# Both conditions' opening modulations on VectorE, and a list schedule with traced durations and a shared port

## The chip, the cores and the metric

The kernel runs on one core of one Trainium2 chip. The metric is the device time of one execution in microseconds. Before the change it is 1679.93 us, the median of three runs (1679.58 to 1681.09). The engines are called PE (TensorE matmuls), PEld (its weight loads), DVE (VectorE), ACT (ScalarE), POOL (GpSimd) and SP (SyncE, whose queue SPq issues nearly all DMAs).

## The reference

Two layers of a diffusion backbone over 512 latent and 256 context tokens of width 1024. Each layer is a token mixer and a gated convolutional FFN, each behind an RMSNorm whose result is modulated with a shift and a scale, and gated. Latent tokens take their modulation from the vector `c`, context tokens from `c_ctx`: both go through the same weights.

```
m  = silu(c) @ w_ada[i] + b_ada[i]                 # shift, scale, gate, twice: 6 x 1024
cm = silu(c_ctx) @ w_ada[i] + b_ada[i]             # the same for the context
h  = rmsnorm(x)  * g * (1 + scale)  + shift
hc = rmsnorm(xc) * g * (1 + cscale) + cshift
layer 0: o, oc = gated linear attention(h, hc)     # 4 heads, decays, state over chunks
layer 1: o     = latent attention(h, hc)           # 8 heads, low-rank keys and values
x = x + gate * o;   x = x + gate2 * conv_ffn(modulate(x))    # context alike, in layer 0
```

The output is the latent stream, (1, 512, 1024) in fp32.

## The kernel before

Activations lie feature-major: a feature tile is 128 features on the partitions by 768 tokens (512 latent, 256 context). Weights and activations are split into a high part (rounded to fp32r by ACT) and a low part (the rest, a subtraction on DVE), and a product is three matmuls: high by high, high by low, low by high. So each weight tile passes a DMA (`ws`), an ACT cast (`wh`) and a DVE subtraction (`wl`), through rings of three buffers, before PE uses it. In the trace all recorded instructions have one line, 263, that of the call that emits them.

The stages are: the opening (`start`, L562), the four heads of gated linear attention (`gla`, L712), the output projection and the first FFN, the latent attention, and the second FFN.

**The opening.** It loads x and the first weights, forms each token's scale `rb` (squares on ACT, sums `sacc` on DVE, `ssq` and `rows` on PE, a power `nr` on POOL), and for each of eight feature tiles makes the two modulations (scale and shift) for the two conditions (`dots`, L623). For tiles 1, 2 and 4 (`MOD_PE`) they are small matmuls `adp`. For tiles 0, 3, 5, 6 and 7 a modulation is a sum over 1024 products of a weight row and the condition, `cb`: in one DVE pass (`junk`, with an accumulator read after it), or, for the entries of `MOD_POOL`, as a product on POOL (`prod`) that ACT then sums. Nine of the twenty are on POOL, all for condition 1, the context; five more entries of the table are of tiles that PE handles and have no effect. Then `normed` scales the tile (DVE writes `x`, ACT writes `hh`, DVE writes `hl`), and PE multiplies it with the first weights: queries `Gq`, keys `Gk`, output gates `mr` and decay gates `mu`, for the latent tokens; the context's products come later, and its last ones go to the bank `both`. Tiles 0 to 7 of x are called x_92 to x_99 in the program, the modulation weights wa_100 (tile 0) to wa_119 (tile 6).

**The heads.** For each head `gates` makes from `Gz` the running sums of log decays (a scan on DVE) and from them `Q` and `K`, for two directions; `values` makes `vps` (copied to `v` by ACT); `core` transposes K (`ktp`, copied to `KT`), makes scores `scp`, states `stp` -> `R` (DVE), outputs `ops`, norms them (`o` on DVE) and transposes them (`Got`). Projections of the next head (`G`) are woven between. In the same stretch 32 modulations of the other chunks are made on DVE and 32 on POOL (`wa<-wa,cb`).

**What sets the order.** `Later` (L102) records each instruction of a stage, and when a pool closes emits all by a list schedule (`flush`, L198): every engine takes the first recorded of the instructions that its own clock shows as ready, with a duration from `cost` (L175) and a delay between engines. Only the order comes out of it; the waits follow from the data. An engine runs its instructions strictly in that order. The costs hold for the whole program: a duration that is too short there puts an instruction into an engine's queue ahead of others that could have run while it waits.

Of the kernel before, what the change touches and what calls it, by code (L numbers as in the profile page):

```python
# [18 lines left out]
P = 128  # L19
# [11 lines left out]
# columns of the vector table  # L31
# [14 lines left out]
# columns of the table of constants  # L46
# [6 lines left out]
# how the start is divided: feature tiles whose first modulations are products of the tensor engine, and  # L53
# (tile, shift or scale, condition) of those whose products GpSimd makes
MOD_PE = (1, 2, 4)
MOD_POOL = (
    (0, 0, 1), (0, 1, 1), (1, 0, 0), (1, 0, 1), (1, 1, 0), (2, 1, 0), (3, 0, 1), (3, 1, 1), (4, 0, 1), (5, 0, 1),
    (5, 1, 1), (6, 0, 1), (7, 0, 1), (7, 1, 1),
)
MOD_STAGE = (0, 1, 2)  # tiles whose modulation weights come in the buffers of the other weights  # L60
# what arrives in turn: modulation weights of a feature tile, two tiles of the first weights, the context
START_LOADS = ("m0", "m1", "w0", "w1", "w2", "m3", "m2", "m5", "m4", "ctx", "w3", "m7", "m6")
COND_AFTER = (3, 7)  # tiles of squares after which the two conditions are taken
CTX_NORM = 5  # the step of the first products at which the norm of the context comes
CTX_LAG = 5  # steps of the context behind those of the latent tokens, not before its norm
NORM_POOL = (3, 6)  # the feature tiles of a latent norm that GpSimd and ScalarE modulate


def weave(*streams):
    """Emits the steps of several streams in proportion: (generator, its expected total, where it starts).  # L70
    A step is its time on the tensor engine, or its share of the total."""
    live = [[g, total, sum(start)] for g, total, *start in streams]
    while live:
        s = min(live, key=lambda x: x[2])
        try:
            step = next(s[0])
            s[2] += step[0] if isinstance(step, tuple) else step / s[1]
        except StopIteration:
            live.remove(s)


def paced(units):
    """Steps of units of work that count as equally long: (generator, its expected total)."""
# [18 lines left out]
class Later:  # L102
    """Records instructions and emits them when a pool ends, in the order of a list schedule.

    Every engine takes the first recorded of the instructions whose operands and buffers are ready; the costs are
    those of the guide. Only the order comes from here: Tile finds all waits anew, in the instructions so ordered."""
# [3 lines left out]
    def __init__(self, tc):  # L110
        self.tc, self.real = tc, tc.nc
        self.ops, self.preload = [], None
        self.seen = {}  # tile -> its accesses in this batch
        self.done = {}  # tile -> when its accesses end, from earlier batches
        self.held, self.tags = {}, {}  # tag, and tile of it -> (tag, the tiles in its buffers)
        self.old = {}  # tile -> the one before in its buffer
        self.free = dict.fromkeys(self.ENGINES, 0.6) | {"sync": 2.2}
        self.table = None
        # from the end of an instruction on one engine to the start of one that needs it on another
# [21 lines left out]
    def record(self, engine, op, args, kw):  # L141
        if op == "preload_act_table_set":
            # goes before the next activation, if that changes the table
            self.preload = args
            return
# [3 lines left out]
        for x, write in aps:  # L149
            row = math.prod(x.tensor.shape[1:])  # L150
            lo = hi = x.offset % row
            # the elements of a partition: from lo to hi, and if they are few, which
# [19 lines left out]
        self.ops.append((engine, op, args, kw, preload, deps, {x.name for x, _ in aps}, *self.cost(engine, op, args, kw, aps)))  # L172

    @staticmethod
    def cost(engine, op, args, kw, aps):  # L175
        """time on the engine, and the activation table"""
# [4 lines left out]
        if engine == "tensor":  # L181
            if op == "transpose":
                return max(0.107, x.shape[-1] / 2400.0), None
            full = (args[1] if len(args) > 1 else kw["lhsT"]).dtype == F32
            return (max(0.213, n / 600.0) if full else max(0.107, n / 2400.0)), None
# [5 lines left out]
        n = max(math.prod(y.shape[1:]) for y, _ in aps)  # L191
        if engine == "vector":
# [3 lines left out]
        return (0.16 * n if kw.get("op") == ALU.pow else 0.1 + n / 450.0), None  # L196

    def flush(self):  # L198
# [6 lines left out]
        # a tile takes the oldest buffer that is no longer in use, and waits for all accesses to the tile there  # L205
# [21 lines left out]
        queue = {e: [] for e in self.ENGINES}  # nothing left to wait for: when ready, which  # L227
        heap = {e: [] for e in self.ENGINES}  # ready by now
# [8 lines left out]
        while any(queue.values()) or any(heap.values()):  # L237
# [6 lines left out]
            cost, table = ops[i][7:]  # L244
# [3 lines left out]
            self.free[e] = end[i] = t + cost  # L248
            plan.append((t, len(plan), i))
# [5 lines left out]
        assert len(plan) == count, "instructions wait for each other"  # L255
# [11 lines left out]
class Net:  # L267
# [36 lines left out]
    def ffn_order(gi):  # L304
        """pairs of a group of FFN features, woven with the down products of the group before"""
# [25 lines left out]
    def ahead(self, n):  # L331
        """n weights after those in use are on their way"""
# [5 lines left out]
    def get(self, key, ahead=2):  # L338
        """the split weights of this key"""
# [6 lines left out]
    def split(self, hi, lo, src, engine=None):  # L346
        """hi + lo == src exactly, each with 12 significant bits."""
# [4 lines left out]
    def weight(self, key, src, shape, pool=None):  # L352
        """split weights, in the ring of 3 or in a pool that keeps them"""
# [1211 lines left out]
def _rope(np):  # L1565
    """cos | signed sin of the axial rotary embedding for the 512 latent tokens"""
    f = 16
# [89 lines left out]
```

## Time and profile before

| what | value |
|---|---|
| median of three runs | 1679.93 us |
| span of the profiled execution, first to last instruction | 1679.1 us |
| PE busy | 1611.4 us, 96% |
| DVE busy | 1116.0 us, 66% |
| ACT busy | 720.4 us, 43% |
| POOL busy | 298.9 us, 18% |
| mean granted clock of TensorE | 0.989 |

The profiled execution is known by its span; the median of the runs lies 0.83 us above it, and so does about what an execution has around its instructions. Busy times are unions over the span, so they don't add up over engines. A matmul's own length in the trace overlaps with that of the next; the distance of two starts says what one costs. A DVE row's length includes any time for which the instruction has been issued and does not get on.

### The profile page before, as it was taken

To read this page: it belongs to the slowest core of one execution; us is meant where nothing else is said; L and a number is where in the kernel's file an instruction comes from. 1 tells how busy PE (TensorE), PEld (TensorE's weight loads), DVE (VectorE), ACT (ScalarE), POOL (GpSimd) and SP (SyncE) were. 2 spreads that over 40 slices of the span, in tenths; PEclk is the share of its full clock that TensorE was granted. 3 is DMA by queue.
4 is the path that set the end of the run, shared out by engine and by line. 5 is a ranking of instruction groups with operands and counts; after the bars stand their busy time and mean duration, and the time that the engine had idled before them with its cause. 6 is when DMAs were issued, how large, how long until landed. Compare 5 with 4: busy or idle time off the path is not lost.

```text
span 1679.1 us, 22918 instructions
## 1 busy us (share of the span) xinstructions
PE 1611.4 (96%) x9086; PEld 1386.0 (83%) x9086; DVE 1116.0 (66%) x1773; ACT 720.4 (43%) x1253; POOL 298.9 (18%) x170
## 2 busy tenths in 40 slices
PE   7899889889999999999999999999999999999999
PEld 4688778778888888888888888788889888888887
DVE  7977777885677855655544567777776765555554
ACT  4555444552443533323322336666653533333331
POOL 3223233330112411111100020334400100000000
PEclk9999999999999999999999999999999999999999
DMA  8222223233133343333331222100031232232232
GB/s 320 99 93 96 93 86 111 76 116 142 38 113 121 131 151 126 126 126 126 126 101 64 76 109 79 40 15 26 20 120 47 69 113 98 90 101 99 90 100 76
DMA packets 50079, 165.59 MB, mean 99 GB/s; under 512 B 5554, under 2 KB 7346, under 8 KB 49972
## 3 DMA queue, kind: packets, MB, share of 16 engines
q1 hardware_dynamic: 49332, 162.04, 28.2%
q0 software_dynamic: 640, 2.10, 0.3%
q8 instruction: 71, 1.16, 0.3%
q14 instruction: 36, 0.29, 0.1%
HBM read 159.92 MB, written 4.19 MB: 98 GB/s over the span
## 4 chain that ended last, share of the span: by engine, by line
PE 78%; DVE 10%; issue 5%; ACT 3%; DMA 2%; POOL 1%; SPq 0%; POOLq 0%; DVEq 0%; ACTq 0%
PE G L263 59%; PE Gs L263 4%; PE av L263 2%; PE ukv L263 2%; DVE K L263 2%; PE Gu L263 2%; DVE junk L263 2%; PE uq L263 1%; DMA wa<-in_wada 1%; PE pt L263 1%; DVE hl L263 1%; PE ops L263 1%; PE vps L263 1%; DVE R L263 1%; PE stp L263 1%
## 5 line engine op out<-in xcount | busy, mean ns | idle before, releaser
L263 PE MATMUL G<-hh,wh 128*128 128x512 f32 (+1 forms) x1416 | 507.0, 358 | 1.2 <-DVE x L263 1.2
L263 PE MATMUL G<-hl,wh 128*128 128x512 f32 (+2 forms) x1416 | 494.1, 350 | 0.2 <-DVE hl L263 0.2
L263 PE MATMUL G<-hh,wl 128*128 128x512 f32 (+1 forms) x1400 | 491.9, 351 | 0.0
L263 DVE TENSOR_TENSOR wl<-ws,wh 128x1024 fp32r<-128x1024 f32 (+3 forms) x178 | 222.4, 1251 | 270.2 <-ACT wh L263 268.7
L263 ACT CAST wh<-ws 128x1024 fp32r<-128x1024 f32 (+3 forms) x186 | 189.5, 1020 | 441.9 <-PE G L263 422.8
L263 PEld LDWEIGHTS G<-hh,wh 128*128 128x128 f32 x1416 | 267.4, 189 | 36.3 <-DVE x L263 1.4
L263 PEld LDWEIGHTS G<-hl,wh 128*128 128x128 f32 (+1 forms) x1416 | 266.7, 188 | 36.9 <-DVE hl L263 0.7
L263 PEld LDWEIGHTS G<-hh,wl 128*128 128x128 f32 x1400 | 264.3, 189 | 34.5
L263 POOL TENSOR_TENSOR wa<-wa,cb 128x1024 f32<-128x1024 f32 x64 | 168.4, 2634 | 524.3 <-DVE mod L263 263.2
L263 PE MATMUL G<-ph,wh 128*128 128x512 f32 (+1 forms) x512 | 181.8, 355 | 2.3 <-DVE z L263 2.3
L263 PE MATMUL G<-ph,wl 128*128 128x512 f32 (+1 forms) x512 | 182.1, 356 | 0.0
L263 PE MATMUL G<-pl,wh 128*128 128x512 f32 (+1 forms) x512 | 181.7, 355 | 0.0
L263 DVE SCALAR_TENSOR_TENSOR z<-G,vec,z 128x511 f32<-128x511 f32 x248 | 151.0, 651 | 1.7 <-ACT z L263 0.9
L263 DVE CUSTOM_DVE_ANT_0 junk<-wa,cb 128x1024 bf16<-128x1024 f32 x75 | 109.9, 1465 | 49.2 <-DMA wa<-in_wada 49.0
L263 PEld LDWEIGHTS G<-ph,wh 128*128 128x128 f32 x512 | 96.2, 188 | 16.9 <-issue 2.6
L263 PEld LDWEIGHTS G<-pl,wh 128*128 128x128 f32 x512 | 96.1, 188 | 14.8
L263 PEld LDWEIGHTS G<-ph,wl 128*128 128x128 f32 x512 | 96.1, 188 | 13.9
L263 ACT ACTIVATE wa<-wa 128x1024 f32<-128x1024 f32 x64 | 67.6, 1057 | 66.4 <-POOL wa L263 66.3
L263 DVE SCALAR_TENSOR_TENSOR x<-G,mod,x 128x512 f32<-128x512 f32 (+1 forms) x112 | 64.8, 610 | 35.2 <-PE G L263 34.7
L263 ACT ACTIVATE z<-G,vec 128x768 f32<-128x768 f32 (+1 forms) x82 | 72.4, 883 | 3.1 <-PE G L263 2.3
L263 ACT ACTIVATE z<-z 128x768 f32<-128x768 f32 (+1 forms) x44 | 32.5, 739 | 93.2 <-DVE z L263 93.2
L263 DVE SCALAR_TENSOR_TENSOR y<-G,mod,y 128x512 f32<-128x512 f32 (+1 forms) x72 | 49.2, 688 | 21.3 <-PE G L263 20.7
(343 smaller groups left out, 2673.0 us busy)
## 6 DMA issues: line engine op xcount, KB each, us to landing
wa<-in_wada SPq DMA_DIRECT2D x90, 512.0 KB, 3.5
ws<-in_wup SPq DMA_DIRECT2D x88, 512.0 KB, 3.3
ws<-in_wdn SPq DMA_DIRECT2D x44, 512.0 KB, 3.5
ws<-in_win SPq DMA_DIRECT2D x13, 512.0 KB, 3.3
ws<-in_wmd SPq DMA_DIRECT2D x9, 512.0 KB, 3.3
ws<-in_wv SPq DMA_DIRECT2D x8, 512.0 KB, 3.7
ws<-in_wog SPq DMA_DIRECT2D x8, 512.0 KB, 3.6
ws<-in_womh SPq DMA_DIRECT2D x8, 512.0 KB, 5.6
```

The lines of the kernel that those rows point to most:

```text
L263: getattr(getattr(self.real, engine), op)(*args, **kw)
```

## The change

Three edits. `MOD_POOL` is empty, so all twenty opening modulations of tiles 0, 3, 5, 6 and 7 are DVE passes. In `start` the pass for condition 1 is recorded right behind that for condition 0 of the same tile (`dots(k, 1)`), not five steps later with the context. And `Later` gets other durations (matmuls some 3 to 8% longer, DVE's scan with about twice its time, POOL's power with a fixed part), and a port: an instruction of DVE or POOL for which `shares` is true starts, in the plan, no earlier than the end of the last such instruction of the other engine. A message for a stuck plan is longer. Comments are gone, so line numbers differ (L263 is L282).

```diff
-MOD_POOL = (
-    (0, 0, 1), (0, 1, 1), (1, 0, 0), (1, 0, 1), (1, 1, 0), (2, 1, 0), (3, 0, 1), (3, 1, 1), (4, 0, 1), (5, 0, 1),
-    (5, 1, 1), (6, 0, 1), (7, 0, 1), (7, 1, 1),
-)
+MOD_POOL = ()
...
+        self.port = {"vector": 0.0, "gpsimd": 0.0}
...
             if op == "transpose":
-                return max(0.107, x.shape[-1] / 2400.0), None
+                return 0.109, None
             full = (args[1] if len(args) > 1 else kw["lhsT"]).dtype == F32
-            return (max(0.213, n / 600.0) if full else max(0.107, n / 2400.0)), None
+            return (max(0.22, n / 590.0) if full else max(0.109, 0.0063 + n / 2296.0)), None
...
+        if op == "tensor_tensor_scan":
+            return 0.07 + n / 480.0, None
...
-        return (0.16 * n if kw.get("op") == ALU.pow else 0.1 + n / 450.0), None
+        return (0.9 + 0.17 * n if kw.get("op") == ALU.pow else 0.1 + n / 450.0), None
+
+    @staticmethod
+    def shares(engine, op, aps):
+
+        reads = [x for x, write in aps if not write and x.space != PSUM and math.prod(x.shape[1:]) > 1]
+        if engine == "gpsimd":
+            return bool(reads) and op != "dma_start"
+        fast = op in ("tensor_scalar", "tensor_copy") and aps[0][0].space != PSUM
+        return engine == "vector" and (len(reads) > 1 or bool(reads) and fast)
...
-            cost, table = ops[i][7:]
+            cost, table, shares = ops[i][7:]
+            if shares:
+
+                t = max(t, self.port[e])
...
             self.free[e] = end[i] = t + cost
+            if shares:
+                self.port["gpsimd" if e == "vector" else "vector"] = t + cost
...
         for k in range(KT + CTX_LAG):
             if k < KT:
                 dots(k, 0)
+                dots(k, 1)
...
             if k >= CTX_LAG:
-                dots(k - CTX_LAG, 1)
                 normed(k - CTX_LAG, 1, *CTX)
```

What this moves is seen in the order of each engine. First DVE in the opening, at feature tile 3: `wa_107` and `wa_108` are its scale and shift weights, `junk` is a modulation pass, `wl` a low part of weights, x_93 and x_95 are feature tiles 1 and 3. Before:

```order
L263 ISA junk,mod_68<-wa_107,cb 128x1024
L263 ISA mod_68 128x1
L263 CAST wh<-wl 128x2x32
L263 ISA junk,mod_68<-wa_108,cb 128x1024
L263 ISA mod_68 128x1
L263 TENSOR_SCALAR mod_68<-adp,vec 128x2 x2
L263 TENSOR_SCALAR gain_123<-mod_68,vec 128x2
L263 TENSOR_TENSOR mod_68<-mod_68,vec 128x2
L263 SCALAR_TENSOR_TENSOR x_93<-x_93,gain_123,rb 128x512
```

The same place on DVE now:

```order
L282 ISA junk,mod_68<-wa_107,cb 128x1024
L282 ISA mod_68 128x1
L282 TENSOR_SCALAR gain_123<-mod_68,vec 128x1
L282 ISA junk,mod_68<-wa_108,cb 128x1024
L282 ISA mod_68 128x1
L282 TENSOR_TENSOR wl<-firsts,wh 128x1024
L282 TENSOR_TENSOR mod_68<-mod_68,vec 128x2
L282 ISA junk,mod_68<-wa_107,cb 128x1024
L282 ISA mod_68 128x1
L282 TENSOR_SCALAR mod_68<-adp,vec 128x2 x2
L282 TENSOR_SCALAR gain_123<-mod_68,vec 128x2
```

A second pass over wa_107 has come in (one over wa_108 follows after x_95), and the weights' low part stands between; POOL's products are gone from its own queue.

Second, PE in the second head, between the transpositions of the keys of the two directions (K_756 and K_762 before, K_738 and K_744 now); `G` are projections of the next head. Before:

```order
L263 MATMUL ktp<-kon,K_756 128x128 x6
L263 MATMUL G<-hl,wh 128x512
L263 MATMUL G<-hh,wl 128x512
L263 MATMUL ktp<-kon,K_762 128x128 x6
L263 MATMUL stp<-v,KT_782 128x256
L263 MATMUL scp<-Q_755,K_756 128x128
```

Now:

```order
L282 MATMUL ktp<-kon,K_738 128x128 x6
L282 MATMUL G<-hh,wh 128x512
L282 MATMUL G<-hl,wh 128x512
L282 MATMUL G<-hh,wl 128x512
L282 MATMUL G<-hh,wh 128x512
L282 MATMUL G<-hl,wh 128x512
L282 MATMUL G<-hh,wl 128x512
L282 MATMUL G<-hh,wh 128x512
L282 MATMUL G<-hl,wh 128x512
L282 MATMUL G<-hh,wl 128x512
L282 MATMUL G<-hh,wh 128x512
L282 MATMUL G<-hl,wh 128x512
```

The second six transpositions (K_744) come only after these eleven projections, one state and 14 more projections, where two stood before. In the fourth head the same pair has 37 projections between them where it had nine.

Third, ACT in the first head, about the second copy of values out of PSUM; `t`, `Q` and `K` are steps of the gates, `wa` sums a POOL product. Before:

```order
L263 ACTIVATE t_666<-t_666 128x768 x2
L263 ACTIVATE cf_663<-cf_663 128x6
L263 ACTIVATE Q_661<-K_662 128x768
L263 ACTIVATE wa,mod_68<-wa 128x1024
L263 ACTIVATE K_662<-K_662 128x768
L263 COPY v<-vps 128x512
```

Now:

```order
L282 ACTIVATE t_648<-t_648 128x768 x2
L282 ACTIVATE wa,mod_68<-wa 128x1024
L282 COPY v<-vps 128x512
L282 ACTIVATE cf_645<-cf_645 128x6
L282 ACTIVATE Q_643<-K_644 128x768
```

The copy has moved ahead of the three steps that wait for DVE's scan; the sum of the POOL product still stands before it.

## Rows read from the trace of the kernel before

**Rows 1.** The page: span; an engine's busy us, share, instructions.

```profile
span 1679.1 us, 22918 instructions
PE   1611.4 (96%) x9086; PEld 1386.0 (83%) x9086; DVE 1116.0 (66%) x1773; ACT 720.4 (43%) x1253; POOL 298.9 (18%) x170
```

**Rows 2.** Windows by stage: length; busy us of each engine; PE clock, DMA share, GB/s.

```profile
13.00:81.20 68.20, 54.57 (x304) 41.49 (x305) 63.02 (x106) 32.69 (x59) 27.09 (x11) 0.97 0.52 195
81.20:384.00 302.80, 271.93 (x1684) 244.44 (x1683) 233.98 (x347) 150.14 (x263) 93.02 (x36) 0.95 0.30 103
384.00:1000.00 616.00, 611.17 (x3529) 537.00 (x3529) 373.21 (x543) 215.69 (x276) 95.86 (x47) 1.00 0.32 109
1000.00:1330.00 330.00, 321.45 (x2041) 276.88 (x2040) 243.26 (x530) 192.68 (x493) 82.48 (x74) 0.99 0.16 51
1330.00:1679.00 349.00, 345.14 (x1528) 283.67 (x1526) 197.74 (x242) 121.32 (x151) 0.00 (x0) 1.00 0.29 95
```

**Rows 3.** POOL's timeline, opening, first head: start, length, instruction, idle before and releaser.

```profile
23.59 2.41 POOL L263 TENSOR_TENSOR prod<-wa,cb 128x1024 f32<-128x1024 f32 x1 [1.85 <-ACT prod L263]
...
64.84 2.61 POOL L263 TENSOR_TENSOR prod<-wa,cb 128x1024 f32<-128x1024 f32 x1 [3.63 <-ACT prod L263]
91.69 3.55 POOL L263 TENSOR_TENSOR wa<-wa,cb 128x1024 f32<-128x1024 f32 x1 [24.23 <-DVE mod L263]
```

**Rows 4.** DVE's timeline, opening.

```profile
13.19 3.44 DVE L263 CUSTOM_DVE_ANT_0 junk<-wa,cb 128x1024 bf16<-128x1024 f32 x1
...
21.56 0.75 DVE L263 SCALAR_TENSOR_TENSOR x<-x,gain,rb 128x512 f32<-128x512 f32 x1 [2.08 <-ACT rb L263]
...
23.64 2.38 DVE L263 TENSOR_TENSOR mod<-mod,vec 128x2 f32<-128x2 f32 x1
...
27.96 1.21 DVE L263 CUSTOM_DVE_ANT_0 junk<-wa,cb 128x1024 bf16<-128x1024 f32 x1
29.11 0.08 DVE L263 DVE_READ_ACCUMULATOR2_ANT mod<- 128x1 f32 x1
...
65.10 2.38 DVE L263 TENSOR_TENSOR mod<-mod,vec 128x2 f32<-128x2 f32 x1
...
70.16 0.74 DVE L263 SCALAR_TENSOR_TENSOR hl<-x,mod,hh 128x512 fp32r<-128x512 f32 x1
```

**Rows 5.** POOL's groups, opening, heads: busy, mean ns; idle before.

```profile
L263 POOL TENSOR_TENSOR prod<-wa,cb 128x1024 f32<-128x1024 f32 x9 | 24.2, 2690 | 30.4 <-ACT prod L263 18.2 <-ACT cb L263 12.3
L263 POOL TENSOR_TENSOR wa<-wa,cb 128x1024 f32<-128x1024 f32 x32 | 86.4, 2701 | 200.7 <-DVE mod L263 170.2 <-ACT t L263 12.8 <-ACT wa L263 6.6
```

**Rows 6.** PE's timeline, opening and heads.

```profile
13.33 1.87 PE L263 MATMUL ssq<-ones,sacc 128*128 128x1 f32 x8 [2.70 <-DVE sacc L263]
...
80.95 0.40 PE L263 MATMUL Gz<-U,w 128*128 128x512 f32 x1
...
99.77 0.41 PE L263 MATMUL vps<-wh,hh 128*128 128x256 f32 x1 [3.12 <-ACT v L263]
...
177.02 1.54 PE L263 MATMUL ktp<-kon,K 128*128 128x128 f32 x6 [4.53 <-DVE K L263]
...
333.87 0.70 PE L263 MATMUL stp<-v,KT 128*128 128x256 f32 x2 [3.40 <-ACT KT L263]
```

**Rows 7.** Windows behind three of these waits, columns as in rows 2.

```profile
100.00:105.00 5.00, 5.00 (x31) 5.00 (x31) 4.01 (x8) 1.90 (x3) 0.00 (x0) 0.66 0.21 79
175.00:180.00 5.00, 2.98 (x13) 2.80 (x13) 4.73 (x5) 2.75 (x7) 1.77 (x2) 0.51 0.18 50
335.00:340.00 5.00, 4.28 (x20) 3.95 (x21) 2.77 (x6) 2.02 (x5) 0.00 (x0) 0.66 0.54 187
```

**Rows 8.** DVE's groups in the heads, columns as in rows 5.

```profile
L263 DVE TENSOR_TENSOR K<-K,k 128x768 f32<-128x768 f32 x8 | 15.6, 1959 | 0.6 <-ACT K L263 0.6
L263 DVE TENSOR_TENSOR_SCAN K<-keep,Q 128x768 f32<-128x768 bf16 x8 | 14.0, 1751 | 0.1
L263 DVE TENSOR_TENSOR K<-K,md 128x768 f32<-128x768 f32 x8 | 7.6, 953 | 0.2
```

More of the change, by code (lines that the diff above doesn't have):

```diff
@@ L171, in record @@
             preload, self.preload = self.preload, None
-        self.ops.append((engine, op, args, kw, preload, deps, {x.name for x, _ in aps}, *self.cost(engine, op, args, kw, aps)))
+        self.ops.append((engine, op, args, kw, preload, deps, {x.name for x, _ in aps}, *self.cost(engine, op, args, kw, aps), self.shares(engine, op, aps)))
     @staticmethod
@@ L254, in flush @@
                     release(j)
-        assert len(plan) == count, "instructions wait for each other"
+        if len(plan) != count:
+            stuck={i for i in range(count) if left[i]>0}
+            i=min(stuck); path=[]
+            while i not in path:
+                path.append(i); i=min(j for j in deps[i] if end[j]==0.0)
+            raise AssertionError("\n".join(f"{i} {ops[i][0]} {ops[i][1]} {sorted(ops[i][6])}" for i in path[path.index(i):]))
         for name, l in users.items():
```

## The prediction

> **What bounds the kernel now.** First the page's totals: PE is busy 1611.4 of 1679.1 us [rows 1], so at most the other 68 us and time at a low clock can be won. Then the windows by stage, which say where those lie [rows 2]: between 384 and 1000 and from 1330 on PE idles 5 and 4 us, and order can do next to nothing there. In the opening (13 to 81.2) PE idles 13.6 us, and DVE is busy 63.0 of 68.2: DVE sets the end there. In the four heads (81.2 to 384) PE idles 30.9 of 302.8 us, at a mean granted clock of 0.95, while DVE is busy 234: neither is full, they wait for each other. In the latent attention (1000 to 1330) PE idles 8.6 us.
>
> Next the timelines of POOL and DVE in the opening, side by side [rows 3, 4]. A pass of DVE over 1024 elements takes 1.21 us, 1.15 from its start to the next instruction (27.96 to 29.11). But an addition on two columns, issued at 23.64, takes 2.38 us and ends at 26.02, when POOL's product (23.59 + 2.41) ends at 26.00; another, issued at 65.10, ends at 67.48, POOL's at 67.45. So a DVE instruction issued while a POOL product runs does not get on until the product ends. Eight of the nine products hold DVE like this, the first in the pass at 13.19 (3.44 us), the last at 65.10; the ninth falls into a wait for `rb`.
>
> **The opening, part by part.** Removed: nine POOL products of 2.69 us [rows 5] and nine ACT sums; neither engine is the bound here, so these count nothing by themselves. What counts is the eight holds on DVE. The pass at 13.19 loses 3.44 - 1.21 = 2.2, the two additions about 2.2 each, and so on: some 2.1 each, 17 us in all. Not all of it comes back: the instruction behind the first pass needs `ssq`, which PE finishes at 13.33 + 1.87 = 15.2 [rows 6], while the pass would end at 14.4, so 1 us stays as idle time. In turn the scale chain begins a good 1 us earlier, and of the wait of 2.08 us for `rb` [rows 4] 1 us goes. Added: nine passes on DVE at 1.15, 10.4 us. Sum: -17 + 1 - 1 + 10.4 = -6.6; I take -7, since going through DVE's new order with these durations puts the last latent tile's `hl` (done at 70.9 now) at 63.5 to 64.5.
>
> Behind that `hl` PE has 10 us of work without a wait now, up to the first gate product at 80.95 [rows 6]; the same products stand there in the new order, so the end of the opening moves with it. What could take the cover away is arrival. SP's queue now holds wa_103, the second load of tile 1, until both passes over wa_100 are done, about 1.4 us later than now, but the third pair of first weights and a tile-3 load have been moved ahead of it and fill the gap. The last load, wa_119, has moved behind two `wv` loads and an x tile, which is some 3 us later; DVE comes to it 7 us earlier than now. DMA is idle after the opening's loads for most of the window (mean share 0.52 [rows 2]), so I allow 1 us for this. Bounds of the opening: -8.5 if all holds and waits go, -4 if arrivals and a second wait for the scale eat 3 us.
>
> The rule that speaks here is in the Trainium skill, "SBUF — State Buffer", section "Who interferes with whom": a DVE instruction with two SBUF inputs, or in a two-port mode, and a POOL instruction that reads SBUF exclude each other for the whole instruction, and the one that issues first blocks the other. The two pairs above agree, POOL first. By the rule POOL can as well be the loser, and then a product on POOL would have cost DVE nothing and the change would add its 10.4 us, 1690; the rows show DVE losing in eight of nine.
>
> **The heads.** Nothing is added or removed here; the order is another. The planner had a scan at 0.87 us, where it takes 1.75 [rows 8], and did not know of the holds, so it put PE's instructions ahead of time behind DVE's. Three places, by the orders shown above.
> (a) PE waits 3.12 us at 99.77 for ACT's copy of `v` [rows 6], which stands behind steps that wait for the scan. Now only the sum of a POOL product is before it, which can begin at 91.69 + 3.55 = 95.2 [rows 3]; the copy is done some 3 us sooner. The clock behind it is 0.66 in five us, that is partly at 1.2 instead of 2.4 GHz, which costs 0.34 x 5 = 1.7 [rows 7]. Together 4.8.
> (b) PE waits 4.53 at 177.02 for K. Now 25 projections come before that instruction instead of two, over 4 us of work. With the clock's 0.49 x 5 = 2.4 behind it: 7.
> (c) 3.40 at 333.87 for the copy of the transposed keys, now covered by 28 more projections, and 1.7 of clock: 5.1.
> These are 17 us. What is moved forward as cover is missing as cover later, and other waits (for `R` and `o`) stay, so I take -15. Bounds: 0, if every gap opens again elsewhere, and -46, all idle time (30.9) and all clock loss (0.05 x 302.8 = 15) of the stage. I take a value nearer to 0 because DVE has 234 us of work that do not shrink, and its chains through scan and decays stay.
>
> **The rest.** In the FFNs PE is full, and its order is nearly the same: 0. In the latent attention the order changes more, but only 8.6 us of idle time are there: 0, plus or minus 2.
>
> **Sum.** 1679.1 - 7 - 15 = 1657.1 for the span; the runs' median lies 0.83 above it, so 1658.
>
> **Rivals.**
> 1. Only the opening pays. Each gap closed in the heads opens later, since DVE limits PE there as a whole. For it: DVE is at 77% of the stage (234 of 302.8) with work in chains; against: three of the longest waits have matmuls ready to go in front of them. 1679.9 - 7 = 1673.
> 2. Nearly all gaps close and the clock stays up: two thirds of the 46 us. For it: every large clock loss follows a wait [rows 6, 7]. 1679.9 - 7 - 30 = 1643.
> 3. Slower: in the heads the 32 POOL products that remain [rows 5] fall on DVE instructions that PE waits for. They hold DVE now too: K<-K,k takes 1.96 us where its like K<-K,md takes 0.95 [rows 8], eight times, so 8 us in that group alone. If all 32 held it for 2.2 us, that would be 70 us. A quarter of the other 62 newly on the way to `ktp` and `ops` is +16, less the opening's 7: 1689. It decides once more than three new holds lie on PE's path. Against it: the plan now knows of the port.
> 4. It does not do what it says: arrivals set the opening's end, or PE's tail is longer, and the heads trade evenly. 1679 to 1680.
>
> **How the numbers follow.** Forecast 0.52 (its own range 1650 to 1666), rival 1 0.20, rival 2 0.12, rival 3 0.08, rival 4 0.08. Faster by over 0.2% (3.4 us, about what a measurement of this kernel can tell from no change) are the first three: 0.84; within 0.2% is rival 4: 0.08; slower is rival 3: 0.08. The range 1643 to 1677 leaves out half of rival 2, rival 3 and most of rival 4, just under 0.2.
>
> **What would show it.** In the changed kernel's opening no small DVE instruction takes over 2 us, there are twenty passes of 1.2 us, the last latent `hl` ends at 63 to 65 and the first `Gz` starts at 73 to 75. In the heads the three waits of (a) to (c) shrink from 11 us to under 4, and the clock of the stage rises from 0.95 to 0.97 or more. I am wrong if `Gz` comes later than 77, if DVE waits for `wa` loads in the opening, or if PE's idle time in the heads stays near 31 us with new releasers.

## The result, and the profile after

The changed kernel takes 1649.86 us (median of 4 runs, 1648.24 to 1651.06) where the kernel before took 1680.14 beside it (1679.58 to 1681.09): a ratio of 0.982, 95% interval 0.9806 to 0.9834. The forecast was 1658 with a range of 1643 to 1677. The total lies in the range, but it is the sum of two terms that were both wrong, in opposite directions, so that it came out so near is in part luck.

The page of the changed kernel, with the lines that answer to [rows 1]:

```profile
span 1649.3 us, 22897 instructions
PE 1606.0 (97%) x9086; PEld 1382.5 (84%) x9086; DVE 1098.8 (67%) x1791; ACT 710.7 (43%) x1235; POOL 273.7 (17%) x161
```

POOL has lost its nine products (25 us). TensorE is busy 5.4 us less with the same 9086 matmuls, though its mean granted clock over the whole span reads 0.989 in both: by stage, below, it is 10.3 us less in the heads and 4.9 more elsewhere. The windows by stage, cut at the same points of the program as [rows 2] (columns as there):

```profile
13.00:81.40 68.40, 57.15 (x304) 43.19 (x304) 54.44 (x123) 21.87 (x39) 3.12 (x2) 0.90 0.54 197
81.40:349.20 267.80, 261.56 (x1691) 236.24 (x1692) 227.37 (x349) 152.57 (x267) 92.29 (x36) 1.00 0.34 116
349.20:965.50 616.30, 611.99 (x3521) 538.83 (x3520) 375.29 (x540) 213.97 (x274) 97.33 (x46) 0.99 0.34 109
965.50:1300.10 334.60, 322.86 (x2039) 278.00 (x2038) 239.32 (x530) 192.83 (x493) 80.73 (x74) 0.98 0.16 50
1300.10:1649.00 348.90, 345.28 (x1528) 283.77 (x1526) 197.91 (x242) 121.55 (x151) 0.00 (x0) 1.00 0.30 95
```

Take the lengths from those of [rows 2]: the opening 68.2 to 68.4, nothing; the heads 302.8 to 267.8, all of the gain and more; the FFNs nothing; the latent attention 330 to 334.6, a loss. In the heads TensorE's idle time fell from 30.9 to 6.2 us and its mean clock rose from 0.95 to 1.00.

DVE's timeline in the opening (start, length, instruction, idle before), against [rows 4]:

```profile
13.46 1.22 DVE L282 CUSTOM_DVE_ANT_0 junk<-wa,cb 128x1024 bf16<-128x1024 f32 x1
...
24.45 0.15 DVE L282 TENSOR_TENSOR mod<-mod,vec 128x2 f32<-128x2 f32 x1
...
32.18 0.35 DVE L282 TENSOR_SCALAR mod<-adp,vec 128x2 f32<-128x2 f32 x2 [2.70 <-PE adp L282]
...
66.00 0.74 DVE L282 SCALAR_TENSOR_TENSOR hl<-x,mod,hh 128x512 fp32r<-128x512 f32 x1
```

The holds (a VectorE instruction that has been issued and doesn't get on while a GpSimd product runs) are gone: the first pass takes 1.22 us where it took 3.44, the addition on two columns 0.15 where it took 2.38. But a new wait of 2.70 us for `adp`, TensorE's modulations of tile 1, is there, and the last latent `hl` ends at 66.7, not at 64. TensorE's timeline says why:

```profile
23.27 0.80 PE L282 MATMUL Gq<-hh,wh 128*128 128x512 f32 x1 [2.88 <-ACT hh L282]
...
29.73 2.13 PE L282 MATMUL adp<-wa,cT 128*2 128x128 f32 x18
...
79.96 0.51 PE L282 MATMUL Gz<-U,w 128*128 128x512 f32 x1 [1.33 <-ACT q L282]
...
82.86 0.39 PE L282 MATMUL vps<-wl,hh 128*128 128x256 f32 x1 [0.88 <-DVE wl L282]
...
96.96 0.39 PE L282 MATMUL vps<-wh,hh 128*128 128x256 f32 x1 [0.29 <-ACT v L282]
...
320.85 0.70 PE L282 MATMUL stp<-v,KT 128*128 128x256 f32 x2 [1.37 <-DVE R L282]
...
1026.31 0.55 PE L282 MATMUL Gkr<-kon,krr 128*128 128x128 f32 x3 [1.68 <-DVE vl L282]
```

At 23.27 it has stood 2.88 us for the first normed tile, and then runs that tile's products partly at 1.2 GHz, so that it comes to the bulk of `adp` only at 29.73; the windows there (columns as in rows 2) show a clock of 0.76 and 0.56:

```profile
20.00:25.00 5.00, 2.12 (x7) 1.25 (x6) 4.26 (x9) 3.10 (x4) 0.00 (x0) 0.76 0.94 335
25.00:30.00 5.00, 5.00 (x17) 2.92 (x17) 4.47 (x9) 0.00 (x0) 0.00 (x0) 0.56 0.99 360
```

At the opening's other end the first `Gz` comes at 79.96 (before 80.95), with new waits for ScalarE behind it; the second `vps` product, at 81.53 in the kernel before, comes at 82.86. On ScalarE's timeline these waits begin with one for the opening's last product:

```profile
78.61 0.60 ACT L282 ACTIVATE og<-mr 128x512 f32<-128x512 f32 x1 [6.34 <-PE both L282]
79.10 0.80 ACT L282 ACTIVATE q<-Gq 128x768 f32<-128x768 f32 x1
```

Of the three places in the heads, (a) waits 0.29 where it waited 3.12 [rows 6]; at (b) and (c) the wait is gone. The 1.37 us for `R` at 320.85 stand before a later state of the fourth head; its first `stp` behind the transposed keys, (c), comes at 300.13 without a wait. The heads' other waits went with them. TensorE's waits in the heads' windows (us in total, times, longest), the five largest before:

```profile
PE ops L263 <- DVE R L263: 8.0, 5, 2.9
PE Got L263 <- DVE o L263: 7.1, 4, 2.0
PE vps L263 <- ACT v L263: 5.8, 2, 3.1
PE ktp L263 <- DVE K L263: 5.7, 2, 4.5
PE stp L263 <- ACT KT L263: 3.4, 1, 3.4
```

And the two largest after:

```profile
PE Got L282 <- DVE og L282: 1.5, 1, 1.5
PE stp L282 <- DVE R L282: 1.4, 1, 1.4
```

### The profile page after: what moved, and what is told of

The parts are those of the page before. It is cut to its first block, busy times and chain, and to the rows that moved or that the text cites. A ratio compares the mean times of both kernels' runs of the same rounds, so it can differ in the third digit from the quotient of the medians.

```text
span 1649.3 us, 22897 instructions
## 1 busy us (share of the span) xinstructions
PE 1606.0 (97%) x9086; PEld 1382.5 (84%) x9086; DVE 1098.8 (67%) x1791; ACT 710.7 (43%) x1235; POOL 273.7 (17%) x161
## 4 chain that ended last, share of the span: by engine, by line
PE 89%; DVE 5%; ACT 3%; POOL 1%; DMA 1%; issue 1%; SPq 0%; POOLq 0%; DVEq 0%; ACTq 0%
PE G L282 65%; PE Gs L282 5%; PE vps L282 3%; PE av L282 2%; PE Gu L282 2%; PE ukv L282 2%; PE uq L282 2%; PE pt L282 1%; PE ops L282 1%; PE stp L282 1%; DVE junk L282 1%; DVE hl L282 1%; DVE wl L282 1%; PE scp L282 1%; PE adp L282 1%
## 5 line engine op out<-in xcount | busy, mean ns | idle before, releaser
L282 PE MATMUL G<-hh,wh 128*128 128x512 f32 (+1 forms) x1416 | 503.2, 356 | 2.1 <-DVE x L282 1.2
L282 PE MATMUL G<-hl,wh 128*128 128x512 f32 (+2 forms) x1416 | 496.4, 351 | 0.5 <-DVE hl L282 0.5
L282 PE MATMUL G<-hh,wl 128*128 128x512 f32 (+1 forms) x1400 | 490.7, 351 | 0.4 <-DVE wl L282 0.4
L282 DVE TENSOR_TENSOR wl<-ws,wh 128x1024 fp32r<-128x1024 f32 (+3 forms) x178 | 225.5, 1268 | 255.8 <-ACT wh L282 253.9
L282 ACT CAST wh<-ws 128x1024 fp32r<-128x1024 f32 (+3 forms) x186 | 189.3, 1019 | 422.9 <-PE G L282 407.3
L282 PEld LDWEIGHTS G<-hh,wh 128*128 128x128 f32 x1416 | 266.3, 188 | 38.8 <-DVE x L282 1.4
L282 PEld LDWEIGHTS G<-hl,wh 128*128 128x128 f32 (+1 forms) x1416 | 266.2, 188 | 35.9 <-DVE hl L282 1.2
L282 PEld LDWEIGHTS G<-hh,wl 128*128 128x128 f32 x1400 | 263.6, 188 | 34.6 <-DVE wl L282 0.8
L282 POOL TENSOR_TENSOR wa<-wa,cb 128x1024 f32<-128x1024 f32 x64 | 171.6, 2684 | 511.3 <-DVE mod L282 222.5
L282 PE MATMUL G<-ph,wh 128*128 128x512 f32 (+1 forms) x512 | 181.9, 355 | 2.8 <-DVE z L282 2.8
L282 PE MATMUL G<-pl,wh 128*128 128x512 f32 (+1 forms) x512 | 182.7, 357 | 0.0
L282 PE MATMUL G<-ph,wl 128*128 128x512 f32 (+1 forms) x512 | 182.3, 356 | 0.0
L282 DVE SCALAR_TENSOR_TENSOR z<-G,vec,z 128x511 f32<-128x511 f32 x248 | 151.2, 651 | 4.2 <-ACT z L282 3.4
L282 DVE CUSTOM_DVE_ANT_0 junk<-wa,cb 128x1024 bf16<-128x1024 f32 x84 | 111.9, 1332 | 60.7 <-DMA wa<-in_wada 60.5
L282 PEld LDWEIGHTS G<-ph,wh 128*128 128x128 f32 x512 | 96.6, 189 | 18.0 <-issue 3.1
L282 PEld LDWEIGHTS G<-pl,wh 128*128 128x128 f32 x512 | 96.8, 189 | 14.2
L282 PEld LDWEIGHTS G<-ph,wl 128*128 128x128 f32 x512 | 96.6, 189 | 13.7
L282 DVE SCALAR_TENSOR_TENSOR x<-G,mod,x 128x512 f32<-128x512 f32 (+1 forms) x112 | 64.9, 610 | 38.2 <-PE G L282 37.8
L282 ACT ACTIVATE wa<-wa 128x1024 f32<-128x1024 f32 x64 | 67.6, 1056 | 52.4 <-POOL wa L282 52.2
L282 ACT ACTIVATE z<-G,vec 128x768 f32<-128x768 f32 (+1 forms) x82 | 72.6, 885 | 16.7 <-PE G L282 16.7
L282 ACT ACTIVATE z<-z 128x768 f32<-128x768 f32 (+1 forms) x44 | 32.6, 740 | 103.1 <-DVE z L282 103.1
L282 DVE SCALAR_TENSOR_TENSOR y<-G,mod,y 128x512 f32<-128x512 f32 (+1 forms) x72 | 49.3, 688 | 19.0 <-PE G L282 18.5
```

The source lines that it names most:

```text
L282: getattr(getattr(self.real, engine), op)(*args, **kw)
```

## The experiments

All runs in one table. The stretches are read from the trace: "heads" here runs from the first `Gz` to the first `Gu`, so it takes in the output projection. Single traces of stretches in which TensorE's order is one and the same differ by 2 to 4 us (the heads of after, e1_planner, e3_pad and e7_best: 325.2 to 327.7), so a difference of that size is read only with the times of the runs beside it.

```
run             first Gz   heads   the rest   median us   ratio to before (95%)
before              80.9   362.4     1235.8     1680.1
after               80.0   327.7     1241.6     1649.9   0.982  (0.9806-0.9834)
e1_planner          89.5   326.0     1236.6     1654.4   0.9848 (0.9822-0.9875)
e2_opening          77.6   360.7     1233.4     1678.2   0.9991 (0.9975-1.0007)
e3_pad              78.0   325.2     1239.0     1645.3   0.980  (0.9774-0.9825)
e4_noport           75.1   358.5     1237.4     1672.1   0.9954 (0.9938-0.9971)
e5_portonly         76.4   332.2     1244.7     1655.1   0.9858 (0.9844-0.9873)
e6_before_dve       82.7   316.1     1234.8     1636.6   0.9746 (0.9731-0.9761)
e7_best             72.8   325.6     1235.5     1635.7   0.9743 (0.9727-0.976)
e8_best_dve         73.6   317.2     1234.9     1629.7   0.9704 (0.9689-0.9719)
e9_simple           75.9   316.0     1236.8     1630.5   0.970  (0.9687-0.9714)
e10_ffn_dve         72.4   317.1     1233.6     1626.1   0.9673 (0.9658-0.9689)
e11_dve_act         80.9   316.9     1236.1     1636.8   0.9748 (0.972-0.9775)
```

**The planner alone, and the opening alone.** The two halves of the change, each put on the kernel before.

```diff
 e1_planner: Later as in the changed kernel, and
+MOD_POOL = ((0, 0, 1), (0, 1, 1), ...)      # as before
+                dots(k - CTX_LAG, 1)        # as before
 e2_opening: Later as in the kernel before, and
+MOD_POOL = ()
+                dots(k, 1)                  # as after
```

> The kernel before with the list schedule's new durations and its shared port alone; the opening's modulations as before (nine products on GpSimd, the second condition five tiles later). Theory: the 30 us are the planner's, since the trace of after has nearly all of TensorE's waits in the heads closed (9 us of idle time where 31 were) and the opening only about 1 us shorter. Then first Gz at 80.5 to 81.5 as in the kernel before, TensorE idle 8 to 12 us in the 300 us behind it, and 1647 to 1653 us. Rival: the faster opening is what lets the heads run without waits, since everything behind it stands ready earlier; then most waits of the heads stay, and the time is 1665 to 1680.

> The kernel before with the modulations of after alone (none on GpSimd, both conditions together); the list schedule's durations as before. Theory: the opening by itself is worth next to nothing, because VectorE's gain there is spent on TensorE at half clock and on the context's products, which all come behind the last latent ones: first Gz at 79 to 81, the heads' waits as before (28 to 33 us of TensorE idle), 1677 to 1681 us. Rival, which is the prediction's term: the opening gives its 7 us, first Gz at 73 to 75, and 1671 to 1675 us.

The heads follow the planner: 326.0 us with it, 360.7 without. The first run's rival, that the opening opens them, falls, and so does the second run's, that the opening gives 7 us: alone it makes no measurable difference. The first run's time, 1654.4 us, lies 1.4 above what its theory had, the second's, 1678.2, within it. Both theories missed the first `Gz`. With the old planner and the new modulations it comes at 77.6, before the 79 that was expected; with the new planner and the old products at 89.5, 9 us late. POOL's and ScalarE's timelines of e1_planner:

```profile
51.55 2.34 POOL L285 TENSOR_TENSOR prod<-wa,cb 128x1024 f32<-128x1024 f32 x1 [9.14 <-DMA wa<-in_wada]
```

```profile
53.92 1.06 ACT L285 ACTIVATE prod<-prod 128x1024 f32<-128x1024 f32 x1 [6.96 <-POOL prod L285]
```

ScalarE's sum stands in the order ahead of a normed tile's `hh`, and waits 6.96 us through POOL for a load. So at the first `Gz` the modulation edit is worth more beside the new planner (89.5 to 80.0) than beside the old one (80.9 to 77.6); of the time, 1654.4 to 1649.9 us, the intervals overlap.

**The wait for og.** One unused tile where the products had theirs:

```diff
             if k == CTX_NORM:
+                st.tile([P, D], F32, tag="prod", name="prod", bufs=1)
```

> The changed kernel with one unused tile of 4 KB a partition in the opening's pool, where the GpSimd products had theirs. Every engine's order is the same as in the changed kernel, to the instruction; only addresses move, and with them the output gate's first write (og<-mr on ScalarE), which without the tile lies where the last weights of the opening lay, waits no more for the products that read them. Theory: the 6.3 us for which ScalarE stood before og hold q, k and the next weights; without it og starts by 73, Gz begins right behind the last product of the opening at 78.5 (it was 79.96), the second vps follows without its 0.88 us wait (it began at 82.86), and the time falls by 2 to 3.5 us, to 1646.5 to 1648. Rival: the wait is covered, since the heads behind it wait for other things; then 1649 to 1650.5 and the same span.

ScalarE's timeline of e3_pad:

```profile
72.99 0.60 ACT L282 ACTIVATE og<-mr 128x512 f32<-128x512 f32 x1
74.79 0.81 ACT L282 ACTIVATE q<-Gq 128x768 f32<-128x768 f32 x1 [1.20 <-PE Gq L282]
```

And TensorE's:

```profile
77.97 0.63 PE L282 MATMUL Gz<-U,w 128*128 128x512 f32 x2
```

The theory holds in the trace: the same instructions in the same order, `og` 5.6 us earlier, `Gz` at 77.97 without a wait, and 4.5 us gained by the first `Gu` (2.0 + 2.5). The median is 4.6 us lower, more than the 2 to 3.5 of the theory, but the two intervals overlap. The pair shows that one unused tile, with every engine's order unchanged, ends the wait of `og` for the opening's last product, so it was a matter of addresses. That `og` had come to lie where the opening's last weights were still being read, since dropping the products' 4 KB tile moved what lay behind it, is the likely reason; no row names an address. The diff doesn't show that either.

**Port or durations.** The planner's two parts, each without the other.

```diff
 e4_noport:
-            return bool(reads) and op != "dma_start"
+            return False
-        return engine == "vector" and (len(reads) > 1 or bool(reads) and fast)
+        return False
 e5_portonly:
-        if op == "tensor_tensor_scan":
-            return 0.07 + n / 480.0, None
-        return (0.9 + 0.17 * n if kw.get("op") == ALU.pow else 0.1 + n / 450.0), None
+        return (0.16 * n if kw.get("op") == ALU.pow else 0.1 + n / 450.0), None
         (and the old durations of matmuls and transposes)
```

> The changed kernel without the shared port in the list schedule (the new durations stay). Theory: the port is the larger piece of the heads' gain, since it tells the planner that VectorE stands still beside each 2.7 us product of GpSimd, which the old plan put in front of copies that TensorE waits for: 10 to 20 us come back as waits in the heads, 1660 to 1670 us. Rival: it is the running sum's duration (1.75 us, planned at 0.87) and the others, and the port hardly matters: 1648 to 1653 us.

> The changed kernel with the list schedule's old durations (matmuls, transposes, GpSimd's powers, and no duration of its own for the running sum); the shared port stays. Taking the port away left the heads as long as before (294 us from the first Gz to the last Got, where the kernel before has 296 and the changed kernel 265). Theory: the port alone does it, and the durations hardly matter: 262 to 269 us for this stretch, 1644 to 1654 us in all. Rival: the planner has to know both, since a running sum planned at half its time puts the port's holds in the wrong place: 275 to 290 us for the stretch, 1658 to 1674 us.

Against 360.7 us with the old planner and the same opening, the durations alone give 2 us (358.5), the port alone 28 (332.2), both 33 (327.7). The port is nearly all of it, more than the first theory had (1672.1 us, where it said 1660 to 1670); the second lands between its two cases (270.9 us from the first `Gz` to the last `Got`, 1655.1 in all), since the durations add some 4.5 us once the port is known. In the opening, though, the plan without the port is the better one: first `Gz` at 75.1.

**The products away from POOL.** If VectorE's holds are the matter, the old plan should do without any change once no product shares the port in the heads.

```diff
 e6_before_dve, on the kernel before:
-  self.ada_dot(wa, layer, chunk, nt, c, None if self.flip or ... else wa)
+  self.ada_dot(wa, layer, chunk, nt, c, None if layer == 0 or self.flip or ... else wa)
 e11_dve_act, on the kernel before:
-            nc.gpsimd.tensor_tensor(prod, wa, self.cb[:, c], op=ALU.mult)
+            (nc.vector if layer == 0 and prod is wa else nc.gpsimd).tensor_tensor(prod, wa, ...)
```

> The kernel before, planner and opening as before, with the heads' 32 products of GpSimd taken by VectorE (layer 0's modulations for the other chunks: both conditions as passes of 1.2 us on VectorE; no product on GpSimd, no summing pass on ScalarE). Theory: the old plan is wrong only in that VectorE stands still beside GpSimd's products; where there are none, it fits, in spite of some 37 us more of passes on VectorE: the stretch from the first Gz to the last Got falls from 296 to 264 to 272 us, TensorE's idle time there from 31 to under 12 us, and the time to 1648 to 1657 us. Rival: the waits come from the order and from the wrong durations, and VectorE gets 37 us more to do: 288 to 305 us for the stretch, 1672 to 1690 us.

> A control to the kernel before with the heads' products on VectorE, which ran at 0.9746 of the kernel before. That edit took away two things at once: the products on GpSimd, and the 32 summing passes on ScalarE that follow them (1.06 us each; ScalarE's busy time from the first Gz to the first Gu fell from 169 to 134 us), and two of the three waits (a) and (c) of TensorE were for ScalarE. Here the products are plain multiplications on VectorE, and ScalarE sums them as before. Theory: the holds are what counts; ScalarE keeps its 169 us, and the stretch from the first Gz to the first Gu is 315 to 325 us (before 362, without both 316), the time 1636 to 1648 us. Rival: ScalarE's freed time is a good part of it; then 335 to 350 us for the stretch and 1655 to 1670 us.

The first goes further than its theory: 250.5 us from the first `Gz` to the last `Got`, where 264 to 272 were expected, and 1636.6 us, 13 below the changed kernel, by one line. The second lands within its theory, with 316.9 us and 1636.8. The heads, 316.1 and 316.9 us, are below the changed kernel's 327.7. The windows of this stretch (columns as in rows 2), of the kernel before, of after, and of the two runs (the last one lies 2 us late, the stretch itself runs from 80.9 to 397.8):

```profile
80.90:443.30 362.40, 329.33 (x2018) 294.70 (x2018) 264.38 (x392) 169.08 (x292) 95.90 (x38) 0.96 0.29 100
```

```profile
80.00:407.70 327.70, 319.78 (x2017) 287.06 (x2018) 255.47 (x392) 171.47 (x294) 93.40 (x38) 0.99 0.33 111
```

```profile
82.70:398.80 316.10, 313.82 (x2019) 284.63 (x2018) 240.94 (x456) 134.12 (x228) 7.83 (x6) 1.00 0.34 115
```

```profile
83.00:399.50 316.50, 313.24 (x2010) 284.40 (x2009) 240.95 (x423) 167.02 (x289) 11.19 (x6) 1.00 0.33 114
```

VectorE (third engine) does 32 passes more in e6_before_dve and is busy 23 us less. Without those passes (32 x 1.22 = 39) it would be 202, so in the kernel before 62 of its 264 us were holds, about 2 us to each of the 32 products; in the changed kernel it was still 53. In e11_dve_act ScalarE keeps its 167 us, and the stretch is as short: it was not ScalarE's summing. Nor was it that ScalarE, in its strict order, waits for GpSimd's products: 37.8 us of the stretch in the kernel before, and 38.7 in the changed kernel, whose stretch is 35 us shorter. Each run has its own schedule, so the orders differ too; that the holds are the cause rests on the port in the plan alone, above, and on the lengths of VectorE's own instructions. DVE's groups (count, busy us, mean ns), of before:

```profile
L263 DVE TENSOR_SCALAR R<-R,cf 128x256 f32<-128x256 f32 x32 | 24.7, 771 | 0.6
...
L263 DVE TENSOR_TENSOR R<-stp,R 128x256 f32<-128x256 f32 x32 | 13.4, 420 | 16.6 <-PE stp L263 16.4
```

Of after:

```profile
L282 DVE TENSOR_SCALAR R<-R,cf 128x256 f32<-128x256 f32 x32 | 31.6, 986 | 0.5
...
L282 DVE TENSOR_TENSOR R<-stp,R 128x256 f32<-128x256 f32 x32 | 13.4, 417 | 6.8 <-PE stp L282 6.6
L282 DVE TENSOR_TENSOR K<-K,k 128x768 f32<-128x768 f32 x8 | 12.0, 1500 | 0.0
```

Of e6_before_dve:

```profile
L263 DVE TENSOR_TENSOR R<-stp,R 128x256 f32<-128x256 f32 x32 | 13.5, 421 | 11.4 <-PE stp L263 11.2
...
L263 DVE TENSOR_SCALAR R<-R,cf 128x256 f32<-128x256 f32 x32 | 11.2, 348 | 0.3
...
L263 DVE TENSOR_TENSOR K<-K,k 128x768 f32<-128x768 f32 x8 | 7.6, 952 | 0.0
```

K<-K,k takes 1959 ns before [rows 8], 1500 after and 952 without products; R<-R,cf even rises from 771 to 986 before it falls to 348. The new plan moves holds from one group to another. R<-stp,R, one of whose two operands is in PSUM, takes the same in all three.

**Putting it together.** e7_best is e3_pad with the port in the plan of the heads and of layer 0's FFN alone; e8_best_dve has the heads' products on VectorE as well; e10_ffn_dve also the FFN's. e9_simple has no change to the planner: e2_opening, the unused tile and the products of e6_before_dve.

```diff
 e7_best, on e3_pad:
+        nc.sharing = False      # from the start's first record to its last, and from layer 1 on
-        ..., self.shares(engine, op, aps)))
+        ..., self.sharing and self.shares(engine, op, aps)))
 e10_ffn_dve, on e8_best_dve:
-  self.ada_dot(wa, layer, chunk, nt, c, None if layer == 0 or self.flip or ... else wa)
+  self.ada_dot(wa, layer, chunk, nt, c)
```

> The changed kernel with the unused 4 KB tile, and with the shared port in the plan of the heads and of layer 0's FFN alone: not in the opening, where the run without the port had its last latent hl at 66.2 us and its first Gz at 75.8 (with the port 71.7 and 78.0), and not from the latent attention on, where the plan with the port has a wait of 1.7 us for vl before Gkr. Theory: both come on top of the tile: first Gz at 74 to 75.5, the heads as with the port (262 to 266 us), the Gkr wait gone; 2.5 to 5 us under the kernel with the tile alone, which ran at 0.980 of the kernel before: 0.9770 to 0.9787. Rival: what the opening gains is lost in the first head, which then waits for weights or for VectorE's backlog: the same 0.979 to 0.981.

> As the run before it (e7), and the heads' 32 products of GpSimd also taken by VectorE, so that no product shares the port in layer 0's heads. Theory: where the plan knows the port, the holds already lie on instructions that TensorE does not wait for, so taking them away gives nothing more: the heads within 3 us of e7's and the same time within 3 us, though VectorE is busy for some 10 us less or more. Rival 1: VectorE, without holds, gives 3 to 6 us more, heads at 258 to 261 us. Rival 2: the 37 us of passes make VectorE late: heads 5 to 15 us longer than e7's.

> No change to the planner at all: the kernel before, with the opening's modulations of after (none on GpSimd, both conditions together), the unused 4 KB tile, and the heads' 32 products on VectorE. Theory: what the planner's new port was worth is had without it where no product is left to share the port: first Gz at 75 to 76.5 (77.6 without the tile), 315 to 318 us from there to the first Gu as in the run of the kernel before with the heads' products on VectorE, and 1627 to 1633 us, 0.969 to 0.972 of the kernel before. Rival: the new durations and the new plan of the opening are worth something of their own beside it; then 3 to 8 us more than the best run so far (1629.7 us, 0.9704): 0.973 to 0.976.

> The best run so far (0.9704 of the kernel before) with the 32 products of GpSimd in layer 0's FFN on VectorE as well (layer 1's modulations). Theory: a hold costs only where TensorE waits for the held instruction; in the FFN it waited 2 to 3 us in 560, so taking the last products away moves nothing: the stretch from the first Gu to cqh stays at 569 to 573 us, and the time within 2 us of 1629.7 (0.969 to 0.9715). Rival 1: the holds cost there too, in gaps too short to show: 4 to 10 us faster. Rival 2: 37 us more passes on VectorE make z or y late: 3 to 10 us slower.

TensorE's timeline of e7_best:

```profile
72.78 0.63 PE L283 MATMUL Gz<-U,w 128*128 128x512 f32 x2
```

In e7_best `Gz` comes at 72.78, below the theory's 74, and the ratio is below its bound too; the wait before `Gkr` shrinks from 1.7 to 0.6 us. (The 75.8 that the expectation gives for the run without the port is its second `Gz`; the first is at 75.1. Its 66.2 and 71.7 are starts of the context's last `hl`, in e4_noport and e3_pad, not of the last latent one.) In e8_best_dve the theory falls and its first rival is right: the time is 6.0 us lower, and the heads lose another 8.4 us, more than the rival said, so the holds that the plan had moved were not free. e9_simple bears out its theory: 316.0 and 0.970, as good as e8_best_dve. In e10_ffn_dve the FFN's stretch (first `Gu` to `cqh`) is 569.7 against 570.9, as the theory said; the median is 3.6 us lower than that of e8_best_dve, more than the theory's 2, and the trace puts no more than 1.2 of it there. The two intervals just touch (0.9689), so whether there is a remainder is open.

## Why the prediction came out as it did

1. *The holds of the opening (-17).* Right: VectorE's small instructions are short again, and twenty passes ran at 1218 ns each.
2. *The opening's sum (-7).* Wrong by 6 to 7 us: -1.0 at the first `Gz`, nothing by the stage's length. Three steps failed. VectorE's new order was walked through with TensorE's modulations taken as ready in time; TensorE ran partly at 1.2 GHz there, the modulations of tile 1 stood behind products for tile 0, and VectorE waited 2.70 us. That "the end of the opening moves with it": from the end of the last latent `hl` to TensorE's last product of the opening it was 10 us before and 12 now. Before, TensorE took that `hl` at once (70.96); now it comes to it at 68.22, 1.5 us after its end, since it had idled and then did the products ahead of it partly at 1.2 GHz (clock 0.86 and 0.80 in the rows below, columns as in rows 2: (0.14 + 0.20) x 5 = 1.7 us). And the wait of `og` cost 2 us at `Gz`; nothing in the instructions' order shows it, it was in the waits. Where these are gone the term is nearly of its size: e7_best, whose opening is planned without the port and so has another order, has its `Gz` at 72.8, where the prediction said 73 to 75; e9_simple, with the old plan, at 75.9. Late loads were no part of it: VectorE waits for no `wa` in the opening.

```profile
60.00:65.00 5.00, 2.80 (x12) 2.32 (x13) 4.72 (x11) 1.15 (x3) 0.00 (x0) 0.86 0.01 3
65.00:70.00 5.00, 5.00 (x23) 4.25 (x23) 5.00 (x15) 2.83 (x6) 0.00 (x0) 0.80 0.00 0
```

3. *The heads (-15).* Mis-sized: -34.7. Rival 2's case is what happened here (its term was -30), and the clock stayed up. Two sentences failed. That "other waits (for `R` and `o`) stay": these two were the largest before, 15.1 us together, and 1.4 for `R` and none for `o` are left. The three places that the prediction counted gave 10.8 of the 24.7 us of idle time that went, and TensorE's busy time, by its clock, fell by 10.3 where the sum had 5.8. And the reason for the lower value, that VectorE "has 234 us of work that do not shrink": some 60 of these were no work but holds. Its busy time did stay, at 227 us, but the plan had moved the holds to where TensorE doesn't wait for them. The prediction had [rows 8] for that, and used them for rival 3 alone.
4. *Which part does it.* The prediction named the running sum's duration first, and the holds second. The runs turn that round: 28 us by the port, 2 by all durations without it, 4.5 on top of it.
5. *Latent attention (0 plus or minus 2).* It lost 4.6 us, more than the 2 allowed: the wait for `vl` before `Gkr` (1.68 us) and smaller ones, at a clock of 0.98 where it was 0.99. From the first `cqh` to the last `Gs` it is 253.5 us before, 257.8 after, and 254.0 in e7_best, where the plan leaves the port out there.
6. *Rival 3.* The chance of 0.08 was for holds that fall on TensorE's path. They still cost TensorE 8 us in the changed kernel's plan (e7_best against e8_best_dve), but far less than in the old one.

The prediction's own tests say the same: "wrong if `Gz` comes later than 77" was met, at 79.96, while all three waits and the clock did better than asked. The span fell by 29.8 us where 22 were forecast: against the forecast by stage, +7 in the opening and +4.6 in the latent attention stood against -20 in the heads.

The rule of the Trainium skill that the prediction weighed ("SBUF — State Buffer", "Who interferes with whom") says also that an instruction of VectorE with at most one input in SBUF, outside its two-port modes, isn't touched. The rows agree: R<-stp,R takes 417 to 421 ns whether POOL works or not, while K<-K,k, with both operands in SBUF, takes 1959 ns beside POOL's products and 952 without. R<-R,cf, a multiplication of one tile, is lengthened too; whether it runs in a two-port mode no run here shows.

## What to carry to other kernels

Before sharing VectorE's work with GpSimd, compare what the operation costs on VectorE with what VectorE stands still for: here 1.22 us against 2, so the offload was a loss that busy shares had hidden as VectorE's own work. A planner that knows of the port wins most of it back by moving the holds, but taking the cause away was better and simpler (0.9746 by one line alone, 0.970 with the opening's modulations and the unused tile, both with the old planner). And after an edit that drops a buffer, compare the waits as well as the order: another tile may have come to lie where something is still being read.

## What the runs showed of the hardware

- Either engine is held by the other, whichever starts second. In the changed kernel a running sum on VectorE began at 91.31 and took its 1.75 us, and POOL's product, which began at 91.62 beside it, took 3.63 us instead of 2.4. VectorE's holds are the other order: the next VectorE instruction, begun at 92.98 while that product ran, took 3.08 us, and 0.96 elsewhere. All 13 products that took over 3.2 us in this kernel began while a VectorE instruction with both operands in SBUF ran.

```profile
91.31 1.75 DVE L282 TENSOR_TENSOR_SCAN K<-keep,Q 128x768 f32<-128x768 bf16 x1
92.98 3.08 DVE L282 TENSOR_TENSOR Q<-Q,t 128x768 f32<-128x768 f32 x1
91.62 3.63 POOL L282 TENSOR_TENSOR wa<-wa,cb 128x1024 f32<-128x1024 f32 x1 [32.69 <-ACT t L282]
```

- Idle time cost TensorE twice here. From the kernel before to the changed one its idle time in the heads' stretch fell by 25.2 us (33.1 to 7.9), and its busy time on the same matmuls by 9.5 (329.3 to 319.8), at a mean clock of 0.96 and 0.99; without the products it is 313.8 at 1.00.
